# Routing on un-normalised rows in a two-layer mixture-of-experts trunk

## The chip, the cores and the metric

The kernel runs on one core of a Trainium2 chip. TensorE (PE) multiplies, VectorE (DVE) and ScalarE (ACT) work on elements, GpSimd (POOL) does small work and issues its own DMA queue with the gathers and scatters, and SyncE (SP) issues the DMAs that load weights. The metric is device time in microseconds, median over runs.

## The reference, cut to what matters

Two layers. Each is a token mixer (layer 0: stick-breaking attention beside retention; layer 1: differential attention), an output projection, a normalised residual, and then a mixture of 32 small experts, two for each token. For 1024 tokens of 1024 features, with folded rows and columns written out:

```python
y   = ALPHA * x + g1 * (mix @ w_out)              # output projection and residual
n   = (y - mean(y)) * rsqrt(var(y) + eps)         # LayerNorm, without gain and bias
x1  = n * lg + lb                                 # residual that the experts' results are added to
u2  = n * sc + sh                                 # rows that the experts read
lgt = n @ (gain * [w_group | w_router]) + br      # 4 + 32 router logits of a token
group = argmax(lgt[:4]); two best of the group's 8 experts; gates by softmax
x2  = LayerNorm(ALPHA * x1 + g2 * sum over the two experts(gate * expert(u2)))
```

An expert is a gated MLP with 512 hidden units. All arithmetic is float32; the matmuls run as three passes over high and low parts.

## The kernel before, in words

A layer has two stages here. In the first, the class `OutProj` computes the output projection in 8 blocks of 128 tokens, as a generator (`gen`) whose steps are laid between those of the mixer's last head. For each block it runs matmuls over 8 slices of the contraction and two halves of the columns (L511); the last block's remaining 12 matmuls come at the end. VectorE scales the result from PSUM (L515) and adds the residual (L517 in layer 1, L519 in layer 0), then takes statistics (L574). `norm` finishes them: bn_aggr (L580), a reciprocal square root in 12 small operations (`rsqrt`, L162 to L171), the negated scaled mean (L583), and then ScalarE normalises the block in place (L584).

From the normalised block come three things:

- `expert_rows` (L598, L599): u2, two VectorE operations over 128 x 1024 and a store by SP's queue;
- `turn` and `logits` (L607, L623): eight transposes on TensorE, two copies by ScalarE, eight matmuls of 36 columns (TensorE shows each as two), and the bias added by VectorE (L625);
- `residual` (L617): x1, two VectorE operations, and a store by POOL's queue (L618).

After every second block `choose` picks group and experts (L634 to L685), `rank` counts by matmul how many earlier tokens each expert has (L693, L695), `hots` and `place` (L701 to L726) put the tokens into a table of slots, and L1644 makes it a table of integers. What a block leaves to do gets a due time in `put_off`: a count of matmul steps of the projection. A scheduler then orders each engine's instructions from this program order and its own cost estimates. `tc.issue_after` adds an ordering and nothing else.

The second stage, `experts`, runs over a list of jobs p. For each, POOL gathers the rows of its tokens (`gather`, L1385) into a buffer from `xgs`, TensorE transposes them (`x_T`, L1396), ScalarE and VectorE split them into high and low parts (L178, L179), and TensorE multiplies with the expert's weights, which stream in 1 MB pieces through a ring of buffers and are split in the same way (L1434 up, L1479 down). The first gather needs the table and all stored u2. Two of the buffers in `xgs` are the tiles `t_v` that hold the two rows lg and lb during the first stage; they come free when the last `residual` has read them, and are cleared by POOL (L1839) ahead of their gather. x1 of blocks 0 to 5 is made as the blocks come; that of block 6 with the last rows, and that of block 7 (`residual(NB - 1)`) has its first operation behind the slot codes (`coded`) and its second behind `plan.behind`: in layer 0 the first job's transposed rows (`es[0].turned`), in layer 1 the counted table (`plan.tabled`).

Of the kernel before, what the change touches and what calls it, by code (L numbers as in the profile page):

```python
# [12 lines left out]
I32 = mybir.dt.int32  # L13
# [21 lines left out]
def tile_trunk(ctx, tc, x, c, ln1_g, ln1_b, ln2_g, ln2_b, w_ada, b_ada,  # L35
# [28 lines left out]
    def bank1():  # L64
        return psB.tile([P, 512], F32, name="psb")
# [93 lines left out]
    def rsqrt(pool, v, n, tag):  # L159
# [12 lines left out]
        return y  # L172

# [209 lines left out]
    class OutProj:  # L383
# [30 lines left out]
        def open(self, pool, mr, uT, u2, g1, extra, arena, lrows, wr):  # L414
# [18 lines left out]
            self.mv = pool.tile([P, NB, 2], F32, name="ln_mv")  # L433
# [5 lines left out]
        def router(self, wr):  # L439

# [15 lines left out]
            nc.vector.tensor_tensor(self.wf, raw, gain, op=OP.mult)  # L456
            self.vals1 = wr[0][:, 0:4 * NE].rearrange("p (k c e) -> p k c e", k=2, c=2)
# [96 lines left out]
        def put_off(self, b, end):  # L554

            g = [g for g in GROUPS if b in g][0]
            todo = [(9, lambda: self.turn(b)), (12, lambda: self.logits(b))]
            if b < NB - 2:
                todo.insert(1, (9, lambda: self.residual(b)))
            elif b == NB - 1:  # L560
                todo.insert(1, (9, lambda: self.last_rows(end)))
            if b == g[-1]:
                todo += [(12, lambda: self.choose(g)), (17, lambda: self.rank(g)), (17, lambda: self.hots(g)),
                         (21, lambda: self.place(g))]
            self.later += [(2 * KT * (b + 1) + n + (13 if b == NB - 2 else 0), f) for n, f in todo]
            self.later.sort(key=lambda t: t[0])
# [9 lines left out]
        def norm(self, b):  # L576
            y = self.y[b % NY]
            st6 = self.small("st6", [2, 6])
            mv = self.mv[:, b, :]
            nc.vector.bn_aggr(mv, st6)  # L580
            rs = rsqrt(self.pool, mv[:, 1:2], 1, "ln")
            nb = self.small("nb", [1])
            end = nc.vector.scalar_tensor_tensor(nb, mv[:, 0:1], -1.0, rs, op0=OP.mult, op1=OP.mult)  # L583
            nc.scalar.activation(y, y, AF.Identity, bias=nb, scale=rs)  # L584
            if b < NB - 2:
                self.expert_rows(b)
            self.put_off(b, end)
# [22 lines left out]
        def residual(self, b):  # L610
            y = self.y[b % NY]
            for i, (t, op) in enumerate(zip(self.lrows, (OP.mult, OP.add))):
                with ExitStack() as st:
                    if b == NB - 1:

                        st.enter_context(tc.issue_after((self.coded, self.rt.plan.behind)[i].ins))
                    nc.vector.tensor_tensor(y, y, t, op=op)  # L617
            nc.gpsimd.dma_start(x1_d[self.l][b * P:(b + 1) * P, :], y)  # L618

        def logits(self, b):  # L620
# [4 lines left out]
            nc.vector.tensor_tensor(self.small("lg", [GM, 36])[:, b - g[0], :], pl[:, 0:36], self.br, op=OP.add)  # L625

        def choose(self, g):
# [44 lines left out]
            nc.vector.tensor_tensor(oh_all[:, b0:b0 + n, :], oh[:, :, 0, :], oh[:, :, 1, :], op=OP.add)  # L672
# [24 lines left out]
        def hots(self, g):  # L697
# [3 lines left out]
            nc.vector.tensor_tensor(rj, self.oh, self.pr[:, 0:n * NE].rearrange("p (b e) -> p b e", b=n).unsqueeze(2)  # L701
                                    .broadcast_to([P, n, 2, NE]), op=OP.mult)
# [1089 lines left out]
    def experts(l, rt, dst):  # L1792

        with ExitStack() as st:
# [68 lines left out]
            rt.op.residual(NB - 1)  # L1863
# [375 lines left out]
```

## Time and profile before

| what | value |
|---|---|
| median of 3 runs | 2659.84 us (2657.39 to 2667.03) |
| profiled execution | 2662.61 us |
| its span, first to last instruction | 2660.9 us |
| PE busy | 2432.1 us (91%) |
| DVE busy | 1788.2 us (67%) |
| ACT busy | 1080.7 us (41%) |
| POOL busy | 341.5 us (13%) |
| mean granted TensorE clock | 0.949 |

The first stage of layer 0 ends near 740 us and that of layer 1 near 1980 us of the span; the experts follow. A busy share of 91% is a mean over stretches that are full and stretches, at the two joints, in which TensorE waits and its clock is lowered, so the joints have to be read by themselves. The median lies 2.8 us below the profiled execution.

### The profile page before, as it was taken

Reading aid. Unit: us, or ns where it says so; the run is one execution under the profiler, and the core shown is the slowest. Engines: PE = TensorE matmul, PEld = TensorE weight load, DVE = VectorE, ACT = ScalarE, POOL = GpSimd, SP = SyncE. Lnnn points to the kernel's source line nnn. Section 1 sums busy time; section 2 is a strip of 40 time slices with the busy share of each in tenths; the row PEclk is TensorE's granted clock in tenths of the full one; section 3 lists DMA queues with packets and bytes.
Section 4 is the critical chain, followed back from the end, with each engine's and each line's share of the span. In section 5 each row is a group of like instructions: output and inputs, shape, how many; then the busy total and the mean of one; then the engine's idle time right before and its main releaser. Section 6 shows DMA issues by size and latency. Waiting matters only on the chain. (4 is left out here: it accounts for less than half of the span.)

```text
span 2660.9 us, 37454 instructions
## 1 busy us (share of the span) xinstructions
PE 2432.1 (91%) x13530; PEld 1800.6 (68%) x13530; DVE 1788.2 (67%) x3659; ACT 1080.7 (41%) x1806; POOL 341.5 (13%) x286
## 2 busy tenths in 40 slices
PE   6999999989889999999879999999979999989995
PEld 5776678877767544445468898987767766656651
DVE  6678987768888564555476778788877545453446
ACT  3344542222267433444354545454226432332331
POOL 1000001110022211222100000000011121121211
PEclk9999999999989999999979999999979999999996
DMA  7534455533579989999833334233268998997983
GB/s 237 146 92 119 120 137 171 170 116 123 206 287 379 369 327 383 388 383 390 315 142 93 92 76 117 64 112 121 101 225 315 372 347 295 408 406 267 381 340 136
DMA packets 216802, 616.65 MB, mean 232 GB/s; under 512 B 31872, under 2 KB 111928, under 8 KB 167457
## 3 DMA queue, kind: packets, MB, share of 16 engines
q1 hardware_dynamic: 193312, 555.96, 57.1%
q0 software_dynamic: 23296, 58.20, 8.7%
q8 instruction: 110, 1.80, 0.3%
q14 instruction: 84, 0.68, 0.1%
HBM read 555.67 MB, written 60.80 MB: 232 GB/s over the span
## 5 line engine op out<-in xcount | busy, mean ns | idle before, releaser
L228 PE MATMUL psb<-w_b,w_sp 128*128 128x512 f32 x1536 | 402.3, 404 | 0.0
L179 DVE TENSOR_TENSOR e_lo<-w_b,e_hi 128x1024 fp32r<-128x1024 f32 x256 | 303.5, 1221 | 79.0 <-ACT e_hi L178 77.3
L178 ACT CAST e_hi<-w_b 128x1024 fp32r<-128x1024 f32 x256 | 261.1, 1047 | 137.9 <-PE psb L1434 71.8
L228 PEld LDWEIGHTS psb<-w_b,w_sp 128*128 128x128 f32 x1536 | 279.9, 191 | 52.5 <-issue 0.7
L248 PE MATMUL psb<-w_sp,w_b 128*128 128x256 f32 x1824 | 248.7, 288 | 0.3
L248 PEld LDWEIGHTS psb<-w_sp,w_b 128*128 128x128 f32 x1824 | 227.7, 191 | 3.2 <-issue 1.2
L1434 PE MATMUL psb<-e_hi,w_sp 128*128 128x512 f32 x592 | 201.6, 410 | 0.6 <-ACT e_hi L178 0.6
L1434 PE MATMUL psb<-e_hi,e_x 128*80 128x512 f32 (+2 forms) x576 | 187.4, 400 | 1.2 <-issue 1.1
L123 DVE SCALAR_TENSOR_TENSOR ada_acc<-ada_slab,cond,ada_acc 128x512 f32<-128x512 f32 x160 | 125.0, 781 | 57.2 <-DMA ada_slab<-in_w_ada_dram 53.9
L511 PE MATMUL psb<-w_b,w_sp 128*128 128x512 f32 x576 | 150.7, 410 | 6.3 <-ACT w_sp L178 6.3
L1492 POOL DMA_INDIRECT x_d<-e_y,tabi x38 | 101.9, 2682 | 411.2 <-DVE e_y L1486 371.7
L1434 PEld LDWEIGHTS psb<-e_hi,w_sp 128*128 128x128 f32 x592 | 115.7, 195 | 31.4 <-ACT e_hi L178 3.5
L1434 PE MATMUL psb<-e_lo,w_sp 128*128 128x512 f32 x320 | 131.0, 409 | 6.5 <-DVE e_lo L179 6.5
L1479 PE MATMUL psa<-e_hi,e_hh 128*128 128x512 f32 (+3 forms) x304 | 128.8, 425 | 4.3 <-ACT e_hi L178 4.1
L1479 PE MATMUL psa<-e_lo,e_hh 128*128 128x512 f32 (+3 forms) x304 | 131.2, 432 | 1.2 <-DVE e_lo L179 1.2
L1322 ACT ACTIVATE df_z<-df_z,df_nm 128x256 f32<-128x256 f32 (+7 forms) x128 | 98.3, 769 | 82.5 <-DVE df_nm L1320 72.0
L1479 PE MATMUL psa<-e_hi,e_hl 128*128 128x512 f32 (+3 forms) x304 | 128.3, 423 | 0.0
L511 PEld LDWEIGHTS psb<-w_b,w_sp 128*128 128x128 f32 x576 | 108.8, 195 | 28.8 <-ACT w_sp L178 6.9
L1434 PE MATMUL psb<-e_lo,e_x 128*80 128x512 f32 (+2 forms) x288 | 116.1, 403 | 11.1 <-DVE e_lo L179 11.1
L1434 PEld LDWEIGHTS psb<-e_hi,e_x 128*80 128x80 f32 (+2 forms) x576 | 96.4, 168 | 38.8 <-issue 2.0
L1385 POOL DMA_INDIRECT t_v<-u_d,tabi x70 | 83.6, 1194 | 230.3 <-PE psa L1512 164.4
L1028 DVE TENSOR_TENSOR_SCAN t_keep<-t_keep,zero 128x128 f32<-128x128 f32 (+7 forms) x64 | 86.7, 1355 | 25.5 <-ACT t_keep L1018 25.1
(544 smaller groups left out, 4729.9 us busy)
## 6 DMA issues: line engine op xcount, KB each, us to landing
w_b<-in_moe_w_dram SPq DMA_DIRECT2D x261, 1024.0 KB
w_raw<-in_moe_w_dram SPq DMA_DIRECT2D x60, 1024.0 KB
w_sp<-in_moe_w_dram SPq DMA_DIRECT2D x44, 1024.0 KB
ada_slab<-in_w_ada_dram SPq DMA_DIRECT2D x160, 256.0 KB
e_ring<-in_moe_w_dram SPq DMA_DIRECT2D x17, 1024.0 KB
w_raw<-in_even_w_in_dram SPq DMA_DIRECT2D x24, 512.0 KB
ada_slab<-in_w_ada_dram SPq DMA_DIRECT2D x16, 512.0 KB
x_d<-w_raw POOLq DMA_DIRECT2D x16, 512.0 KB, 3.1
```

The costliest lines, as they stand in the source:

```text
L123: nc.vector.scalar_tensor_tensor(acc, slab, cond[:, k:k + 1], acc, op0=OP.mult, op1=OP.add)
L178: nc.scalar.copy(hi, src)
L179: return eng.tensor_tensor(lo, src, hi.bitcast(F32), op=OP.subtract)
L228: nc.tensor.matmul(ps, s[:, k % 4, cs], m[:, k, :], start=k == 0 and j == 0, stop=k == KT - 1 and j == 2)
L248: nc.tensor.matmul(ps[:, t, :], s[:, k, sl], m[:, k % 4, :], start=k == 0 and j == 0, stop=k == KT - 1 and j == 2)
L511: nc.tensor.matmul(pss[b][n], m[:, s, k, :], self.wo[k][:, w, ns], start=k == 0 and j == 0, stop=k == KT - 1 and j == 2)
L1028: nc.vector.tensor_tensor_scan(R[:, ::-1], R[:, ::-1], zero1.broadcast_to([P, W]), 1.0, OP.mult, OP.add)
L1322: nc.scalar.activation(pm[m][:, 0:W], pm[m][:, 0:W], AF.Exp, bias=nm[:, m:m + 1], accum_out=H.ss[:, qb, m:m + 1])
L1385: self.gathered = nc.gpsimd.indirect_dma_start(out=xg[0:m], out_offset=None, in_=u2_d[self.l], in_offset=bass.IndirectOffsetOnAxis(ap=tab[ ...
L1434: self.upped = nc.tensor.matmul(ps[0:n], s[:, ks], wt[:, ws], start=k == 0 and j == 0, stop=k == KT - 1 and j == len(sms) - 1)
L1479: nc.tensor.matmul(pn, s[:, ks], w[:, ns], start=k == 0 and j == 0, stop=k == 3 and j == 2)
L1492: nc.gpsimd.indirect_dma_start(out=x1_d[self.l], out_offset=bass.IndirectOffsetOnAxis(ap=tab[0], axis=0), in_=y, in_offset=None, bounds_ch ...
```

## The change

The router works on y itself, not on n. As the mean times a column sum is what the normalisation takes away, the columns of the weights are made free of their mean once for each layer (three more VectorE operations, one matmul), and the logits are then rs * (y @ wf) + br, with rs the reciprocal square root of the token. ScalarE's normalising pass is gone. The rows u2 and x1 take the norm in with them: (y - mean) * row0, then * rs + row1, as two operations that read a scalar of each token and a second tensor (`row_step`). The reciprocal square root of a block has 9 small operations instead of 12 and L583.

The due times are smaller (turn 3, logits 6, rows 6, residual 9; before 9, 12, none, 9), and block 6's are put off by 7, not 13. The rows of blocks 6 and 7 and their residuals, which stood together behind block 7's norm, now stand in different places: rows of block 6 behind block 7's reciprocal square root, rows of block 7 behind the choice (`chosen`) and ahead of `hots`, the first residual operation of block 6 behind `coded`, and the other three behind `plan.behind`.

```diff
+            nc.vector.tensor_reduce(s, self.wf.rearrange("p k n -> p n k"), axis=AX.X, op=OP.add)
+            nc.tensor.matmul(ps[:, 0:36], ones, s, start=True, stop=True)
+            nc.vector.tensor_scalar(s, ps[:, 0:36], -1.0 / D, None, op0=OP.mult)
+            nc.vector.tensor_tensor(self.wf, self.wf, s.unsqueeze(1).broadcast_to([P, KT, 36]), op=OP.add)
...
-            todo = [(9, lambda: self.turn(b)), (12, lambda: self.logits(b))]
+            todo = [(3, lambda: self.turn(b)), (6, lambda: self.logits(b))]
             if b < NB - 2:
-                todo.insert(1, (9, lambda: self.residual(b)))
-            elif b == NB - 1:
-                todo.insert(1, (9, lambda: self.last_rows(end)))
+                todo += [(6, lambda: self.expert_rows(b)), (9, lambda: self.residual(b))]
+            if b == NB - 1:
+                todo += [(6, lambda: self.last_rows(NB - 2, self.scaled))]
             if b == g[-1]:
+                todo += [(12, lambda: self.choose(g))]
+                if b == NB - 1:
+                    todo += [(12, lambda: self.last_rows(NB - 1, self.chosen))]
...
         def norm(self, b):
-            rs = rsqrt(self.pool, mv[:, 1:2], 1, "ln")
-            end = nc.vector.scalar_tensor_tensor(nb, mv[:, 0:1], -1.0, rs, op0=OP.mult, op1=OP.mult)
-            nc.scalar.activation(y, y, AF.Identity, bias=nb, scale=rs)
+            self.rs[b], self.scaled = rsqrt1(self.rt.pool, mv[:, 1:2], f"ln{b % 2}")
...
+        def row_step(self, i, b, out_, y, rows):
+            if i == 0:
+                return nc.vector.scalar_tensor_tensor(out_, y, self.mv[:, b, 0:1], rows[0], op0=OP.subtract, op1=OP.mult)
+            return nc.vector.scalar_tensor_tensor(out_, out_, self.rs[b], rows[1], op0=OP.mult, op1=OP.add)
...
-            rt.op.residual(NB - 1)
+            rt.op.residual(NB - 2, (rt.op.coded, plan.behind))
+            rt.op.residual(NB - 1, (plan.behind, plan.behind))
```

The lines move: L584 is gone, and the changed kernel's L533 is L511 of before (matmuls of the projection), L628 is L607 (transposes), L643 and L645 are L623 and L625 (logits and what finishes them), L614 and L615 are the two row steps in place of L598, L599 and L617, L638 is L618 (store of x1), L1409 is L1385 (gather), L1863 is L1839 (clearing a gather's buffer).

Three places show what moves. First TensorE at the end of layer 0's projection, before: w_b are its weights, w_sp the mixed heads, w_raw the rows y, t_q their transposes, ada_slab the router's weights.

```order
L511 MATMUL psa<-w_b_5510,w_sp 128x512 [waits Activation_49]
L511 MATMUL psa<-w_b_5510,w_sp 128x512
L511 MATMUL psa<-w_b_5510,w_sp 128x512 [waits DVE_49]
L511 MATMUL psa<-w_b_5509,w_sp 128x512 [waits DVE_49]
L511 MATMUL psa<-w_b_5509,w_sp 128x512 x5
L511 MATMUL psa<-w_b_5510,w_sp 128x512 x6
L607 MATMUL psb<-identf,w_raw 128x128 [waits Activation_49]
L607 MATMUL psb<-identf,w_raw 128x128 x3
L607 MATMUL psb<-identf,w_raw 128x128 [waits PE_49]
L607 MATMUL psb<-identf,w_raw 128x128 x3
L623 MATMUL psb<-ada_slab,t_q 128x36 [waits Activation_49]
```

The same place in the changed kernel:

```order
L1104 MATMUL psb<-identf,t_k 128x128 [waits PE_49]
L643 MATMUL psb<-ada_slab,t_q 128x36 [waits DVE_49,Activation_49]
L643 MATMUL psb<-ada_slab,t_q 128x36 x3
L643 MATMUL psb<-ada_slab,t_q 128x36 [waits Activation_49]
L643 MATMUL psb<-ada_slab,t_q 128x36 x2
L533 MATMUL psa<-w_b_5510,w_sp 128x512 [waits Activation_49]
L533 MATMUL psa<-w_b_5510,w_sp 128x512
L533 MATMUL psa<-w_b_5510,w_sp 128x512 [waits DVE_49]
L643 MATMUL psb<-ada_slab,t_q 128x36
L533 MATMUL psa<-w_b_5509,w_sp 128x512 [waits DVE_49]
L533 MATMUL psa<-w_b_5509,w_sp 128x512 x5
L533 MATMUL psa<-w_b_5510,w_sp 128x512 x6
```

The last 12 projection matmuls (two rows, of 5 and 6, with one before them) stood ahead of block 6's transposes and logits; now block 6's logits, and its transposes above the rows shown, stand ahead of them, and so does a transpose of the head.

Second, VectorE between block 7's reciprocal square root and the choice of layer 0, before: t_qw is the output of u2 rows, w_sp and t_v the folded rows, t_g small tiles, psb the logits in PSUM.

```order
L583 SCALAR_TENSOR_TENSOR t_g<-ln_mv,ln_i 128x1 [waits DVE_49]
L598 TENSOR_TENSOR t_qw<-w_raw,w_sp 128x1024 [waits DMAHW2_49]
L599 TENSOR_TENSOR t_qw<-t_qw,w_sp 128x1024 [waits DVE_49]
L598 TENSOR_TENSOR t_qw<-w_raw,w_sp 128x1024 [waits Activation_49]
L617 TENSOR_TENSOR w_raw<-w_raw,t_v 128x1024
L599 TENSOR_TENSOR t_qw<-t_qw,w_sp 128x1024 [waits DVE_49]
L617 TENSOR_TENSOR w_raw<-w_raw,t_v 128x1024 [waits DVE_49]
L625 TENSOR_TENSOR t_g<-psb,ada_slab 128x36 [waits PE_49]
L634 TENSOR_REDUCE t_g<-t_g 128x2 [waits DVE_49]
L636 TENSOR_TENSOR t_g<-t_g 128x8 [waits DVE_49]
```

In the changed kernel:

```order
L186 SCALAR_TENSOR_TENSOR ln_i<-ln_t,ln_i 128x1 [waits DVE_49]
L614 SCALAR_TENSOR_TENSOR t_qw<-w_raw,ln_mv,w_sp 128x1024 [waits DMAHW2_49]
L645 SCALAR_TENSOR_TENSOR t_g<-psb,ln_i,ada_slab 128x36 [waits DVE_49,PE_49]
L615 SCALAR_TENSOR_TENSOR t_qw<-t_qw,ln_i,w_sp 128x1024 [waits DVE_49]
L655 TENSOR_REDUCE t_g<-t_g 128x2 [waits DVE_49]
L657 TENSOR_TENSOR t_g<-t_g 128x8 [waits DVE_49]
```

Six row operations stood between the norm and the logits of block 7; now it is one, and one more behind the logits, ahead of the choice's first operation. The two rows of block 7 have moved behind the choice and the residual steps further down.

Third, POOL's queue at the start of layer 0's experts, before: u_d holds the rows u2, t_v are gather buffers, x_d holds x1.

```order
L1385 DMA t_v<-u_d_72,tabi_133 128x1024 [waits DMAHW3_49,DMAHW4_49,DMAHW2_49,DMAHW6_49,DMAHW1_49,DMAHW7_49,DMASW7_49,DVE_49]
L1846 MEMSET mark_6925 128x1 [waits DMAHW0_49,DMAHW5_49,PE_49,DMAHW6_49,Activation_49,Pool_49]
L1839 MEMSET t_v 128x1024
L1677 MEMSET pl_ones 32x128
L1385 DMA t_v<-u_d_72,tabi_133 128x1024 [waits DMASW0_49,Pool_49]
L1385 DMA t_v<-u_d_72,tabi_133 128x1024 [waits DMASW7_49,DMASW1_49,PE_49]
L1839 MEMSET t_v 128x1024 [waits DVE_49]
L618 DMA x_d_78<-w_raw 128x1024 [waits DMASW2_49]
L1385 DMA t_v<-u_d_72,tabi_133 128x1024 [waits DMASW3_49,Pool_49]
```

In the changed kernel:

```order
L1409 DMA t_v<-u_d_72,tabi_133 128x1024 [waits DMAHW4_49,DMAHW3_49,DMAHW5_49,DMAHW2_49,DMAHW6_49,DMAHW1_49,DMAHW7_49,DMASW6_49,DVE_49]
L1870 MEMSET mark_6887 128x1 [waits DMASW7_49,PE_49,DMAHW0_49,Activation_49,Pool_49]
L1701 MEMSET pl_ones 32x128
L1409 DMA t_v<-u_d_72,tabi_133 128x1024 [waits DMASW6_49,PE_49]
L638 DMA x_d_78<-w_raw 128x1024 [waits DMASW0_49,DVE_49]
L1863 MEMSET t_v 128x1024 [waits DVE_49]
L1409 DMA t_v<-u_d_72,tabi_133 128x1024 [waits DMASW1_49,Pool_49]
L1863 MEMSET t_v 128x1024 [waits DVE_49]
L638 DMA x_d_78<-w_raw 128x1024 [waits DMASW2_49]
L1409 DMA t_v<-u_d_72,tabi_133 128x1024 [waits DMASW3_49,Pool_49]
```

The second gather, that of job 1, stood right behind the first with its buffer cleared in between; it is now the one behind the first L1863, which waits for VectorE, and both the gather that waits for TensorE and the store of block 6's x1 stand ahead of it. The first gather is the first row in both, the gather that waits for TensorE the one with PE in its waits.

## Rows read from the trace of the kernel before

**Rows 1.** Windows: us, busy (x instructions) of PE, PEld, DVE, ACT, POOL; PEclk, DMA share, GB/s

```profile
680.00:700.00 20.00, 19.96 (x108) 16.88 (x106) 17.38 (x49) 4.79 (x6) 0.53 (x1) 1.00 0.30 97
720.00:740.00 20.00, 11.93 (x71) 10.34 (x69) 15.23 (x53) 4.83 (x8) 0.53 (x1) 0.67 0.93 356
...
800.00:850.00 50.00, 50.00 (x236) 37.61 (x235) 44.22 (x42) 35.03 (x38) 8.85 (x6) 1.00 1.02 381
1960.00:1980.00 20.00, 11.10 (x79) 10.39 (x78) 16.50 (x66) 4.35 (x7) 1.06 (x2) 0.55 0.72 268
```

**Rows 2.** PE's waits, 700 to 760 us: us in total, times, longest

```profile
PE psb L693 <- DVE oh_all L672: 5.5, 2, 3.6
PE psa L1396 <- DMA t_v<-u_d,tabi: 4.7, 1, 4.7
PE psb L607 <- ACT w_raw L584: 4.0, 1, 4.0
```

**Rows 3.** PE's waits, 1815 to 1945 us

```profile
PE psb L607 <- ACT w_raw L584: 2.3, 1, 2.3
```

**Rows 4.** Timeline of PE, end of layer 0's projection: start, us, [idle before <-releaser]

```profile
717.57 5.46 PE L511 MATMUL psa<-w_b,w_sp 128*128 128x512 f32 x12 [1.51 <-DVE w_raw L519]
722.85 1.06 PE L607 MATMUL psb<-identf,w_raw 128*128 128x128 f32 x8
724.20 1.97 PE L623 MATMUL psb<-ada_slab,t_q 128*128 128x36 f32 x16 [0.29 <-ACT t_q L608]
732.03 3.63 PE L623 MATMUL psb<-ada_slab,t_q 128*128 128x36 f32 x16
...
759.67 1.06 PE L1396 MATMUL psa<-identf,t_v 128*128 128x128 f32 x8
```

**Rows 5.** Timeline of DVE, 724 to 756 us

```profile
724.52 0.69 DVE L574 BATCH_NORM_STATS2 t_g<-w_raw 128x6 f32<-128x512 f32 x1
...
735.93 0.16 DVE L634 TENSOR_REDUCE t_g<-t_g 128x2 f32<-128x8 f32 x1
...
738.94 0.23 DVE L672 TENSOR_TENSOR oh_all<-t_g 128x64 bf16<-128x64 f32 x1
...
739.82 0.29 DVE L701 TENSOR_TENSOR t_g<-t_g,psb 128x128 f32<-128x128 f32 x1
...
751.13 1.23 DVE L179 TENSOR_TENSOR e_x<-psa,e_x 128x1024 fp32r<-128x1024 f32 x1 [2.46 <-ACT e_x L178]
```

**Rows 6.** DVE, all operations of L851 (two tensors, one scalar): ns min/median/max, first to last start

```profile
L851 DVE SCALAR_TENSOR_TENSOR ada_acc<-ada_slab,cond,ada_acc x16: 1274/1284/3243, 9.1 to 41.5; 128x1024 f32<-128x1024 f32 x16
```

**Rows 7.** Timeline of POOL, 742 to 757 us

```profile
743.59 1.09 POOL L1385 DMA_INDIRECT t_v<-u_d,tabi  x1 [6.98 <-DMA w_raw<-in_moe_w_dram]
...
753.54 0.95 POOL L1839 MEMSET t_v<- 128x1024 f32 x1 [2.23 <-DVE w_raw L617]
...
755.35 1.33 POOL L1385 DMA_INDIRECT t_v<-u_d,tabi  x1 [0.31 <-issue]
```

**Rows 8.** L1385, issued 740 to 800 us: from issue to landing

```profile
DMA to landing us min/median/max: 4.4/8.4/13.5
```

**Rows 9.** L1385, issued 755 to 756 us: from issue to landing

```profile
DMA to landing us min/median/max: 7.4/7.4/7.4
```

**Rows 10.** Timelines of DVE, POOL and PE, layer 1, 1955 to 2001 us

```profile
1957.62 0.69 DVE L574 BATCH_NORM_STATS2 df_q<-w_raw 128x6 f32<-128x512 f32 x1
...
1969.62 0.16 DVE L634 TENSOR_REDUCE df_q<-df_q 128x2 f32<-128x8 f32 x1
...
1992.56 0.19 DVE L1713 TENSOR_REDUCE pl_full<-pl_v 128x1 f32<-128x32 f32 x1
...
1996.07 1.06 POOL L1385 DMA_INDIRECT t_v<-u_d,tabi  x1 [0.17 <-POOL bt_iota L1580]
...
1999.16 1.05 PE L1396 MATMUL psa<-identf,t_v 128*128 128x128 f32 x8
```

**Rows 11.** L1385, issued 1996 to 1997 us: from issue to landing

```profile
DMA to landing us min/median/max: 9.3/9.3/9.3
```

More of the change, by code (lines that the diff above doesn't have):

```diff
@@ L172, in rsqrt, with rsqrt1 @@
         return y
+    def rsqrt1(pool, v, tag):
+        nh = pool.tile([P, 1], F32, name=tag + "_h")
+        nc.vector.tensor_scalar(nh, v, EPS, -0.5, op0=OP.add, op1=OP.mult)
+        yi = pool.tile([P, 1], I32, name=tag + "_i")
+        nc.vector.tensor_scalar(yi, nh.bitcast(I32), 1, None, op0=OP.arith_shift_right)
+        nc.vector.tensor_scalar(yi, yi, -1.0, float(0x5F3759DF - 0x400000 - 0x40000000), op0=OP.mult, op1=OP.add)
+        y = yi.bitcast(F32)
+        t = pool.tile([P, 1], F32, name=tag + "_t")
+        for _ in range(3):
+            nc.vector.tensor_scalar(t, y, y, nh, op0=OP.mult, op1=OP.mult)
+            end = nc.vector.scalar_tensor_tensor(y, t, 1.5, y, op0=OP.add, op1=OP.mult)
+        return y, end
     rsqrt_end = [None]
@@ L432, in open @@
             self.router(wr)
-            self.mv = pool.tile([P, NB, 2], F32, name="ln_mv")
+            self.mv = self.rt.pool.tile([P, NB, 2], F32, name="ln_mv")
+            self.rs = {}
             self.arena = [(t, [0]) for t in arena]
@@ L608, in turn, with residual @@
                 nc.scalar.copy(uT[:, 4 * h:4 * h + 4, :].rearrange("p k t -> p (k t)"), pt)
-        def residual(self, b):
+        def residual(self, b, behind=(None, None)):
             y = self.y[b % NY]
-            for i, (t, op) in enumerate(zip(self.lrows, (OP.mult, OP.add))):
+            for i in range(2):
                 with ExitStack() as st:
-                    if b == NB - 1:
-                        st.enter_context(tc.issue_after((self.coded, self.rt.plan.behind)[i].ins))
-                    nc.vector.tensor_tensor(y, y, t, op=op)
+                    if behind[i]:
+                        st.enter_context(tc.issue_after(behind[i].ins))
+                    self.row_step(i, b, y, y, self.lrows)
             nc.gpsimd.dma_start(x1_d[self.l][b * P:(b + 1) * P, :], y)
@@ L624, in logits @@
             g = [g for g in GROUPS if b in g][0]
-            nc.vector.tensor_tensor(self.small("lg", [GM, 36])[:, b - g[0], :], pl[:, 0:36], self.br, op=OP.add)
+            nc.vector.scalar_tensor_tensor(self.small("lg", [GM, 36])[:, b - g[0], :], pl[:, 0:36], self.rs[b], self.br,
+                                           op0=OP.mult, op1=OP.add)
         def choose(self, g):
@@ L2154, in route @@
         rt = Route()
+        rt.pool = pool
         rt.plan = Plan(l, rt, pool, NSTAT[l], SIZES[l])
```

36 lines of the change are left out of this document (16 added, 20 removed).

## The prediction

> **What bounds the kernel now.** I read the windows first. Inside the first stage and in the experts TensorE is full: 19.96 of 20 us in 680 to 700, all 50 us in 800 to 850, where the DMA engines are full as well (share 1.02) [rows 1]. At the two joints it isn't: 11.93 of 20 us at a granted clock of 0.67 in 720 to 740, and 11.10 at 0.55 in 1960 to 1980 [rows 1]. A change of norm and routing acts on the time there, or where TensorE waits for the norm inside the first stage. The waits say for what: at the joint of layer 0 it waits 5.5 us for the choice (longest 3.6), 4.7 for the first gathered rows and 4.0 for ScalarE's normalising pass [rows 2]; among the earlier blocks I count one wait for that pass worth naming, 2.3 us in layer 1 [rows 3]. Then the timelines give the chain of the joint. Block 7's rows y are complete when its statistics start, at 724.52; the choice starts at 735.93, its result is there at 738.94, the first gather is issued at 743.59, and job 1's rows are transposed at 759.67 [rows 4, 5, 7]. VectorE, not TensorE, sets 735.93: six row operations run between the norm and the logits, though TensorE ends the logits at 735.66 as well, because its clock is low (the 16 logits matmuls of block 7 take 3.63 us, those of block 6 1.97) [rows 4].
>
> **The change part by part.** All sums are in the profiled execution, 2662.61 us, of which 1.7 lie outside the span; the median of the runs is 2.8 lower, and so is my forecast for it.
>
> *Blocks 0 to 5.* The ACT pass and four small operations of a block leave the path to the transposes. Worth at most the 2.3 us of [rows 3]; the mean-free weights add three small operations and a matmul per layer, ahead of the first block where VectorE has time, at most 1 us if uncovered. The 64 row operations become a form with two tensors and a scalar. The same form over 128x1024 takes 1.284 us in L851 [rows 6]; a plain two-tensor operation of that size takes 1.23 [rows 5]. So 64 times 0.05 is 3 us on VectorE, in stretches where it has 17.38 of 20 us taken and TensorE is full [rows 1]: hidden. I take -1.5, between -2.3 and +1.
>
> *Joint of layer 0, up to the first gather.* Block 6's transposes and logits, 722.85 to 726.17, so 3.3 us [rows 4], now stand ahead of the last 12 projection matmuls. These took 5.46 us at the low clock, behind a wait of 1.51 [rows 4]. With that work in the wait's place I expect them at the upper level, near half, 2.7 us. Complete rows y then come 0.6 later (725.1); at the low clock 3.3 later (727.8). I take 725.8. From there, turn and logits of block 7 take 3.3 us as block 6's did at the upper clock. VectorE beside it has the statistics (0.69) and some eleven small operations at about 0.2 with their gaps (L634 is 0.16 long) [rows 5], 2.9 us together by this estimate, and one row operation of block 6, until 730.0. So the logits are finished at 730.2, the second row operation of block 6 follows (1.28), and the choice starts at 731.5 instead of 735.93: -4.4. With TensorE at the low clock it would be about -3.
>
> Two row operations of block 7 now stand between the choice's result and the use of the ranks: 2 x 1.28 + 0.3 where 0.88 passed before (738.94 to 739.82 [rows 5]), so +2.0. The table and the first gather come 2.4 earlier, at 741.2. But block 7's store, and the 3 MB of weights that wait for it, leave about 3 us later than before, so they run beside the gather. It landed in 4.4 us; the five gathers of this stretch took 4.4 to 13.5, median 8.4 [rows 8]. I take 6.4: the first rows are transposed only 0.4 earlier.
>
> *Joint of layer 0, the second gather.* This is where the change adds a wait. Job 1's buffer is one of the tiles that hold lg and lb. Before, its clearing and gather came right behind the first. Now the tile is read until block 7's first residual operation, which is placed behind the first job's transposed rows. Block 6's second operation and block 7's first run behind the split e_x (751.13 [rows 5], now 750.7): 1.2 + 2 x 1.28, so until 754.5. Then POOL clears the buffer (0.95 [rows 7]) and issues at 755.5, past the store of block 6's x1, which stands ahead in its queue. Behind this gather there wait a clearing, the second x1 store and the next gather. The gather that POOL issued at 755.35 took 7.4 us [rows 9]; with that, job 1's rows are there at 762.9. TensorE asked for them at 759.67 [rows 4]; the new order puts three matmuls more ahead of it (0.7 us, by their rate of 0.23 at the upper clock), so its own time would be 760.4. Late by +2.5 against before. By 4.4 us it would be no loss (-0.4), by 13.5 it would be +8.6. Three row operations among the splits of e_lo, where one stood, cost up to 2.6 us on VectorE; they delay the first job's matmuls ahead of the same gather, so they are no term of their own.
>
> *Joint of layer 1.* The choice started at 1969.62, 12.0 us after block 7's rows were complete (1957.62) [rows 10]. Now block 6's transposes and logits (3.3) stand ahead of the 12 matmuls, which makes 1960.9, and 5.7 us later, as in layer 0, the choice: 1966.6, so -3.0, and +2.0 for block 7's rows: -1.0. Between -2.3 and +1.5, the upper end with TensorE at the low clock. The second gather waits here for the counted table (last operation 1992.56 [rows 10], now 1991.7), two row operations (2.6) and a clearing (0.95): issue at 1995.3. That is the place of the gather of 1996.07, which took 9.3 us [rows 10, 11]: 2004.6. TensorE transposed job 1's rows at 1999.16 [rows 10], now some 1.1 later for matmuls moved ahead. Late by +4.3; by 4.4 us -0.6, by 13.5 +8.5.
>
> *Sum.* Joints +6.8. TensorE and the DMA engines are both full in the experts [rows 1], so no view says which of them carries a late start to the end: if TensorE, all of it; if the weights, that go on filling their ring meanwhile, less. I let 5 of 6.8 through. -1.5 + 5 = +3.5: 2666.1 for the profiled execution, 2663 for the median.
>
> **The rivals.** *A, the joints pay.* Both gathers land about as fast as the first one, 4.4 us. Then layer 0 gets its 2.4, layer 1 its 1.0, the blocks 2.3: -5.7, so 2654. For it: the late gathers are issued when the 3 MB are mostly in. Against it: four of the five gathers in the stretch were slower than that one, which went first [rows 8].
>
> *B, POOL's queue piles up, slower.* The second gather now goes out beside x1 stores, a weight piece on the same queue and the ring's pieces. If gathers there take 13.5 us, the slowest seen [rows 8], TensorE's stall is +8.6 in layer 0 and +8.5 in layer 1, all carried: 2676. It decides from landings of some 12 us on, in both layers. Against it: the gathers at just these places took 7.4 and 9.3.
>
> *C, the row operations run at half rate.* The L851 row gives 1.284 us for 1024 elements of each partition, as fast as the plain form to 5% [rows 6]. The Trainium skill (Vector Engine (DVE) Microarchitecture Reference, section 7, Points that are easy to get wrong) says that a scalar-tensor-tensor with two non-bf16 sources in SBUF runs at half throughput. By that rule the operation would take twice what a two-tensor one takes; L851's sources are two f32 tensors too, and its row disagrees with it here. Were the row steps at 2.5 us all the same, 64 of them would add 79 us to VectorE, which has 2.6 us of 20 free in the first stage [rows 1]; with half of it hidden, 2700.
>
> **How the numbers follow.** My forecast 60%, its own range 2657 to 2669 (the late gathers 2 us faster or 2.5 us slower in both layers). A 27%, B 11%, C 2%. The range takes in A with its spread down to 2650 and goes up to 2672, where B's lower part begins; B's rest, C and the low edge of A stay outside. 0.5% is 13.3 us, about what a measurement tells from no change: below 2646.5 or above 2673.1. Faster by that needs both joints at their lower bounds (-3.1 or so each), the blocks at theirs and more: 4%. Slower: most of B and C and a little of my own case's tail, 11%. The rest, 85%, lies within.
>
> **What would show it.** Right: TensorE has no wait for ScalarE ahead of L628 any more; layer 0's choice (L655) starts near 6 us behind block 7's complete rows, where 11.4 passed before; the first gather goes out 1 to 3 us earlier; TensorE waits 2 to 5 us at L1420 for job 1's rows in both layers, and the gathers there have landed 7 to 10 us after their issue. L614 and L615 take near 1.28 us. Wrong: no wait for job 1's rows (then A), landings of 12 us and a wait for job 2's rows as well (B), L614 over 2 us (C). If the 12 matmuls still run at 0.455 us each, my time for the choice is too early by 2 to 3 us; if the start of the experts moves by 5 us and the end doesn't, it was the weights that set the end.

## The result, and the profile after

| | before | changed kernel |
|---|---|---|
| median of 5 runs, us | 2659.84 (2657.39 to 2667.03) | 2685.60 (2676.64 to 2688.58) |
| profiled execution, us | 2662.61 | 2676.64 |
| span, us | 2660.9 | 2674.9 |

The ratio of the times is 1.0072, 95% interval 1.0046 to 1.0097: slower by some 19 us, and above the forecast's whole range. (The quotient of the two medians, 1.0097, is higher.) The changed kernel's five times fall into two groups, 2676.64 and 2676.69 and then 2685.60 to 2688.58; the profiled execution is of the first, 9 us below the median.

The first row of the statistics in each layer's projection cuts the span into parts that can be compared. VectorE's timeline of before:

```profile
609.67 0.69 DVE L574 BATCH_NORM_STATS2 t_g<-w_raw 128x6 f32<-128x512 f32 x1
...
1830.51 0.69 DVE L574 BATCH_NORM_STATS2 df_q<-w_raw 128x6 f32<-128x512 f32 x1
```

From there to there it is 1220.84 us, and 830.4 from the second row to the end of the span. VectorE's timeline of the changed kernel, with the joint of layer 0 between the two rows and that of layer 1 behind them:

```profile
605.54 0.69 DVE L598 BATCH_NORM_STATS2 t_g<-w_raw 128x6 f32<-128x512 f32 x1
...
719.82 0.69 DVE L598 BATCH_NORM_STATS2 t_g<-w_raw 128x6 f32<-128x512 f32 x1
...
725.30 0.15 DVE L655 TENSOR_REDUCE t_g<-t_g 128x2 f32<-128x8 f32 x1
...
728.29 0.22 DVE L693 TENSOR_TENSOR oh_all<-t_g 128x64 bf16<-128x64 f32 x1
...
737.48 0.16 DVE L1662 MEMSET few_o<- 64x1 f32 x2 [2.06 <-DMA u_d<-t_qw]
...
749.61 1.22 DVE L194 TENSOR_TENSOR e_lo<-w_b,e_hi 128x1024 fp32r<-128x1024 f32 x1
750.74 1.28 DVE L615 SCALAR_TENSOR_TENSOR w_raw<-w_raw,ln_i,t_v 128x1024 f32<-128x1024 f32 x1
751.94 5.76 DVE L194 TENSOR_TENSOR e_lo<-w_b,e_hi 128x1024 fp32r<-128x1024 f32 x5
...
1836.10 0.69 DVE L598 BATCH_NORM_STATS2 df_q<-w_raw 128x6 f32<-128x512 f32 x1
...
2002.59 5.76 DVE L194 TENSOR_TENSOR e_lo<-w_b,e_hi 128x1024 fp32r<-128x1024 f32 x5
```

Layer 0's part takes 1230.56 us now, 9.7 more, and layer 1's 838.8, 8.4 more: 18 us, most of them, by the next table, lost where the experts begin. (What precedes 605.54 is not touched by the change and came 4.1 us earlier in this execution.) The 8.4 is no measure of what layer 1 loses: from job 4's rows, in the last line of the next table, to the end of the span it is 597.6 us here and 603.6 before. The work there is the same; TensorE's mean granted clock is not, 0.91 before and 0.96 after in these two windows, each 400 us behind those rows, before and then after (columns as in [rows 1]):

```profile
2457.00:2537.00 80.00, 73.90 (x399) 50.02 (x392) 37.77 (x40) 29.34 (x38) 15.90 (x11) 0.91 0.99 376
```

```profile
2477.00:2557.00 80.00, 77.55 (x432) 52.35 (x435) 36.69 (x38) 29.23 (x38) 15.98 (x11) 0.96 0.99 385
```

Why it differs is open. The places of the joint, each counted from the layer's first statistics:

| us from the layer's first statistics | layer 0 before | after | layer 1 before | after |
|---|---|---|---|---|
| block 7's rows y complete (its statistics start) | 114.9 | 114.3 | 127.1 | 131.3 |
| choice starts | 126.3 | 119.8 | 139.1 | 137.2 |
| first gather issued | 133.9 | 133.0 | 149.0 | 149.3 |
| first job's rows transposed | 138.4 | 137.5 | 152.9 | 152.5 |
| job 1's rows transposed | 150.0 | 160.4 | 168.7 | 180.8 |
| later job (job 3 in layer 0, job 4 in layer 1) | 182.0 | 193.5 | 226.8 | 241.2 |

Up to the first job nothing is lost; between the first job and job 1 it is 11 to 13 us in each layer. TensorE's waits of the changed kernel (us in total, times, longest), layer 0's joint and then layer 1's, say for what:

```profile
PE psa L1420 <- DMA t_v<-u_d,tabi: 18.7, 2, 10.8
PE psb L714 <- DVE oh_all L693: 8.5, 2, 5.3
...
PE psa L1420 <- DMA t_v<-u_d,tabi: 12.1, 2, 11.1
```

Gathered rows cost 18.7 us in two waits where they cost 4.7 in one [rows 2]. The second of the two is job 1's, as TensorE's timeline shows in both layers:

```profile
713.99 4.34 PE L533 MATMUL psa<-w_b,w_sp 128*128 128x512 f32 x12 [1.40 <-DVE w_raw L541]
...
743.03 1.97 PE L1420 MATMUL psa<-identf,t_v 128*128 128x128 f32 x8 [7.88 <-DMA t_v<-u_d,tabi]
...
765.90 1.97 PE L1420 MATMUL psa<-identf,t_v 128*128 128x128 f32 x8 [10.79 <-DMA t_v<-u_d,tabi]
...
2016.90 1.95 PE L1420 MATMUL psa<-identf,t_v 128*128 128x128 f32 x8 [11.15 <-DMA t_v<-u_d,tabi]
```

Before, it transposed these rows when it came to them [rows 4, 10]. POOL's timeline of the changed kernel holds the reason:

```profile
738.50 1.10 POOL L1409 DMA_INDIRECT t_v<-u_d,tabi  x1 [41.00 <-DVE pl_gt L1690]
...
745.28 1.05 POOL L1409 DMA_INDIRECT t_v<-u_d,tabi  x1 [5.42 <-PE psa L1420]
748.79 0.60 POOL L638 DMA_DIRECT2D x_d<-w_raw  x1 [2.47 <-DVE w_raw L615]
749.76 0.95 POOL L1863 MEMSET t_v<- 128x1024 f32 x1 [0.36 <-DVE w_raw L614]
750.98 7.63 POOL L1409 DMA_INDIRECT t_v<-u_d,tabi  x1 [0.27 <-POOL t_v L1863]
758.60 0.97 POOL L1863 MEMSET t_v<- 128x1024 f32 x1
759.50 0.60 POOL L638 DMA_DIRECT2D x_d<-w_raw  x1
760.40 1.05 POOL L1409 DMA_INDIRECT t_v<-u_d,tabi  x1 [0.30 <-issue]
...
2001.63 7.63 POOL L1409 DMA_INDIRECT t_v<-u_d,tabi  x1 [0.27 <-POOL t_v L1863]
```

Job 1's gather begins at 750.98, 12.5 us behind the first; before it was 2.4. And the instruction itself takes 7.63 us, where the first takes 1.10, in both layers alike. It ends at 758.61 and 2009.26; VectorE's row of five e_lo splits, shown above, ends at 757.70 and 2008.35: 0.91 us earlier, in both. The landings of these two gathers, from the start of the instruction:

```profile
DMA to landing us min/median/max: 14.9/14.9/14.9
...
DMA to landing us min/median/max: 15.1/15.1/15.1
```

Counted from the end of the instruction that is 7.3 and 7.5 us, between the 6.1 and 8.2 that the gathers of [rows 7, 9] and [rows 10, 11] give in the same way (7.4 less 1.33, 9.3 less 1.06). Windows of the changed kernel, same stretches and columns as [rows 1]:

```profile
680.00:700.00 20.00, 19.96 (x102) 16.75 (x101) 17.34 (x34) 2.23 (x4) 1.06 (x2) 1.00 0.36 136
720.00:740.00 20.00, 6.46 (x63) 5.83 (x63) 15.34 (x65) 3.79 (x7) 1.36 (x3) 0.59 0.98 388
```

ScalarE has 2.23 us where it had 4.79, VectorE as much as before: the norm left ScalarE and cost VectorE nothing here.

### The profile page after: what moved, and what is told of

Read it like the earlier page. It is cut to its first block, busy times and chain, and to the rows that moved or that the text cites. A ratio compares the mean times of both kernels' runs of the same rounds, so it can differ in the third digit from the quotient of the medians.

```text
span 2674.9 us, 37387 instructions
## 1 busy us (share of the span) xinstructions
PE 2424.3 (91%) x13534; PEld 1795.8 (67%) x13534; DVE 1782.4 (67%) x3601; ACT 1062.4 (40%) x1790; POOL 363.8 (14%) x286
## 5 line engine op out<-in xcount | busy, mean ns | idle before, releaser
L1516 POOL DMA_INDIRECT x_d<-e_y,tabi x38 | 109.4, 2878 | 402.7 <-DVE e_y L1510 363.1
L533 PE MATMUL psb<-w_b,w_sp 128*128 128x512 f32 x576 | 150.6, 407 | 4.9 <-ACT w_sp L193 4.9
L1409 POOL DMA_INDIRECT t_v<-u_d,tabi x70 | 99.0, 1415 | 296.0 <-PE psa L1536 158.6
L1458 PE MATMUL psb<-e_lo,e_x 128*80 128x512 f32 (+2 forms) x288 | 116.9, 406 | 11.1 <-DVE e_lo L194 11.1
L533 PEld LDWEIGHTS psb<-w_b,w_sp 128*128 128x128 f32 x576 | 107.0, 193 | 26.3 <-ACT w_sp L193 5.4
```

The source lines that it names most:

```text
L533: nc.tensor.matmul(pss[b][n], m[:, s, k, :], self.wo[k][:, w, ns], start=k == 0 and j == 0, stop=k == KT - 1 and j == 2)
L1409: self.gathered = nc.gpsimd.indirect_dma_start(out=xg[0:m], out_offset=None, in_=u2_d[self.l], in_offset=bass.IndirectOffsetOnAxis(ap=tab[ ...
L1458: self.upped = nc.tensor.matmul(ps[0:n], s[:, ks], wt[:, ws], start=k == 0 and j == 0, stop=k == KT - 1 and j == len(sms) - 1)
L1516: nc.gpsimd.indirect_dma_start(out=x1_d[self.l], out_offset=bass.IndirectOffsetOnAxis(ap=tab[0], axis=0), in_=y, in_offset=None, bounds_ch ...
```

## The experiments

Times are medians, each compared with the kernel before on the same chip; every interval is for 95%.

| run | us | before | ratio | y complete, L0 / L1 | job 1's rows, L0 / L1 |
|---|---|---|---|---|---|
| changed kernel | 2685.60 | 2659.84 | 1.0072 [1.0046, 1.0097] | 114.3 / 131.3 | 160.4 / 180.8 |
| e1 | 2664.87 | 2663.46 | 1.0008 [0.9993, 1.0022] | 115.7 / 132.5 | 150.2 / 170.1 |
| e2 | 2680.19 | 2663.46 | 1.0062 [1.0040, 1.0083] | 117.6 / 132.5 | 155.1 / 174.2 |
| e3 | 2679.51 | 2663.46 | 1.0053 [1.0034, 1.0073] | 116.4 / 127.9 | 152.0 / 166.1 |
| e4 | 2652.63 | 2663.46 | 0.9958 [0.9945, 0.9971] | 108.8 / 123.5 | 143.4 / 160.7 |
| e5 | 2653.63 | 2664.51 | 0.9964 [0.9950, 0.9978] | 108.6 / 123.4 | 143.3 / 160.9 |
| e6 | 2650.34 | 2664.51 | 0.9944 [0.9931, 0.9958] | 108.7 / 123.8 | 144.0 / 162.8 |
| e7 | 2667.81 | 2664.51 | 1.0012 [1.0001, 1.0023] | 116.9 / 132.6 | 151.8 / 172.4 |
| e8 | 2650.03 | 2664.51 | 0.9944 [0.9931, 0.9957] | 108.7 / 123.8 | 143.2 / 162.0 |

The last two columns are counted as in the table above.

**e1: only block 7's first residual operation goes back behind the slot codes.**

```diff
-            rt.op.residual(NB - 1, (plan.behind, plan.behind))
+            rt.op.residual(NB - 1, (rt.op.coded, plan.behind))
```

> The changed kernel with one edit: block 7's first residual operation stands behind the slot codes again, so that the buffer of job 1's gather is free early. Theory 1 (the loss is job 1's gather: its buffer is held by block 7's residual, and then POOL's gather instruction is kept up by VectorE's row of split operations): the gather instruction takes 1.0 to 1.4 us instead of 7.63, TensorE waits under 2 us for job 1's rows in both layers instead of 10.8 and 11.1, and the time is 2645 to 2660, below before by up to 12. Theory 2 (the loss is in the new row operations or their places on VectorE): no gain, 2673 to 2690. Theory 3 (gathers land late in this stretch whatever their place, from the weights' traffic): TensorE still waits 5 us or more for job 1's rows; 2665 to 2680.

The loss is gone, 1.0072 to 1.0008, though not in the range that theory 1 had (2645 to 2660): this run is level with before, not below. TensorE has no wait for job 1's rows in either layer. POOL's timeline of layer 0 has job 1's gather 2.4 us behind the first again, at its usual length:

```profile
744.51 1.10 POOL L1409 DMA_INDIRECT t_v<-u_d,tabi  x1 [40.90 <-DVE pl_gt L1690]
...
746.93 1.06 POOL L1409 DMA_INDIRECT t_v<-u_d,tabi  x1 [0.17 <-POOL pl_ones L1701]
```

The place of one VectorE operation, whose result only the second residual operation and the store of x1 need, is worth about 17 us. The operation itself takes 1.28 us in each layer, so most of that is what waits for the buffer that it reads. In layer 1 the gain is smaller: job 4's rows come 235.7 us behind the first statistics, where the changed kernel has 241.2 and before 226.8. Job 2's gather is held there for 5.47 us, and TensorE waits 5.5 us for it.

**e2: the splits of e_lo are kept off the gather.** The buffer is still held, but VectorE's row of splits starts only behind a mark that POOL writes after job 1's gather.

```diff
+                if p == 1:
+                    with tc.issue_after(es[1].gathered.ins):
+                        nc.gpsimd.memset(mark[2], 0.0)
+                    plan.second = nc.vector.tensor_copy(mark[3], mark[2])
...
-                            st.enter_context(tc.issue_after(E.turned.ins))
+                            st.enter_context(tc.issue_after(plan.second.ins))
```

> The changed kernel, with the splits of job 0's remaining weights placed behind job 1's gather on VectorE (a small mark that POOL writes behind the gather and VectorE copies). The buffer is held as long as in the changed kernel; only VectorE's unbroken row of operations no longer runs beside the gather. Theory 1 in its second half (VectorE keeps up the gather instruction): it takes 1.0 to 1.4 us on POOL instead of 7.63, lands 4 to 9 us after its issue instead of 14.9, TensorE's wait for job 1's rows falls to 1 to 5 us in each layer, and the time to 2660 to 2672 though VectorE idles some 2 us. Rival (the instruction waits for room in the DMA queue behind the x1 store, or for something in memory): it stays near 7.6 us and the time at 2675 to 2692.

POOL's timeline (job 1's gather of layer 0, job 2's of layer 1), and then TensorE's waits of layer 0 and of layer 1 and its timeline in layer 1:

```profile
757.82 1.06 POOL L1409 DMA_INDIRECT t_v<-u_d,tabi  x1 [0.31 <-issue]
...
2001.94 1.47 POOL L1409 DMA_INDIRECT t_v<-u_d,tabi  x1 [0.30 <-issue]
```

```profile
PE psb L1458 <- DVE e_lo L194: 2.7, 1, 2.7
...
PE psb L1458 <- DVE e_lo L194: 4.2, 1, 4.2
```

```profile
2018.32 0.48 PE L1420 MATMUL psa<-identf,t_v 128*128 128x128 f32 x1 [9.70 <-DMA t_v<-u_d,tabi]
```

Job 1's gather takes 1.06 us with VectorE quiet and lands in 4.4 (layer 1: 1.07 and 4.2), so without the row of splits beside it, it isn't held. (It need not be held beside one: the next gather, at 760.16, took 1.06 beside four splits.) The time, though, hardly moved: TensorE now waits for the later splits and, in layer 1, 9.7 us for the rows of job 2. Their gather goes out 24 us behind the first instead of 17, and it lands late as well, with a short instruction:

```profile
DMA to landing us min/median/max: 16.3/16.3/16.3
```

The expectation of the time was missed. As the later splits are this run's own cost, it doesn't tell what the long instruction alone is worth; e3 has the hold without it.

**e3: the kernel before with that hold and nothing else.**

```diff
-                        st.enter_context(tc.issue_after((self.coded, self.rt.plan.behind)[i].ins))
+                        st.enter_context(tc.issue_after(self.rt.plan.behind.ins))
```

> The kernel before with one edit: block 7's first residual operation stands behind the first job's transposed rows (layer 0) or the counted table (layer 1), as in the changed kernel; all else as before. Theory 1: this alone makes the loss. Job 1's gather goes out 8 to 12 us later than before in layer 0, its instruction takes 4 to 8 us, TensorE waits 6 to 14 us for job 1's rows in each layer; 2672 to 2692. Theory 2 (the loss is in the row operations and where they stand): within 5 us of before, 2655 to 2665.

It loses 0.53%, without the new norm, router or due times. POOL's timeline in layer 1 and TensorE's wait there:

```profile
1995.82 1.86 POOL L1385 DMA_INDIRECT t_v<-u_d,tabi  x1 [0.27 <-POOL t_v L1839]
...
2012.20 0.54 POOL L1368 DMA_DIRECT2D w_raw<-in_moe_w_dram  x1 [8.78 <-DMA x_d<-w_raw]
2013.04 1.78 POOL L1385 DMA_INDIRECT t_v<-u_d,tabi  x1 [0.31 <-issue]
```

```profile
PE psa L1396 <- DMA t_v<-u_d,tabi: 13.6, 2, 11.5
```

The time is as theory 1 had it, but not by its steps: job 1's gather takes only 1.86 us (expected 4 to 8), and TensorE waits 0.5 us for job 1's rows in layer 0 and 2.1 in layer 1 (expected 6 to 14). What is late is the queue behind it. A weight load on POOL's queue waits 8.78 us for a store of x1, and job 2's gather stands behind it, 30 us behind the first gather instead of 17. TensorE waits 11.5 us for it.

**e4: norm and router alone.** The changed kernel's `rsqrt1`, `row_step` and mean-free router, with the due times and the places of the last rows of before.

```diff
-            todo = [(3, lambda: self.turn(b)), (6, lambda: self.logits(b))]
+            todo = [(9, lambda: self.turn(b)), (12, lambda: self.logits(b))]
...
-                    todo += [(12, lambda: self.last_rows(NB - 1, self.chosen))]
...
-            rt.op.residual(NB - 2, (rt.op.coded, plan.behind))
-            rt.op.residual(NB - 1, (plan.behind, plan.behind))
+            rt.op.residual(NB - 1, (rt.op.coded, plan.behind))
```

> The changed router, reciprocal square root and row operations, but with the due times and the places of the last blocks' rows and residuals of the kernel before. Theory 1: no loss; the wait of TensorE for ScalarE's normalising pass is gone (4.0, 4.3 and 2.3 us before), the row operations of blocks 6 and 7 still hold up the choice; 2652 to 2660. Theory 2 (the row operations cost the time): 2668 to 2690.

It is 0.42% faster than before, about 11 us, and the gain comes earlier than at the joint: rows y are complete 6.1 us sooner in layer 0 and 3.6 in layer 1. TensorE's timeline of before, ahead of [rows 4]:

```profile
710.88 0.18 PE L693 MATMUL psb<-oh_all,trib 128*128 128x32 bf16 x1 [1.93 <-DVE oh_all L672]
...
712.62 0.65 PE L724 MATMUL psb<-t_g 128*128 128x64 f32 x2 [1.32 <-DVE t_g L708]
```

That is the ranking of blocks 4 and 5, for which TensorE waits 1.93 and 1.32 us; the 12 matmuls behind it then take 5.46 [rows 4]. In e4:

```profile
706.49 0.19 PE L716 MATMUL psb<-oh_all,trib 128*128 128x32 bf16 x1
...
714.40 3.01 PE L533 MATMUL psa<-w_b,w_sp 128*128 128x512 f32 x12
```

No wait for the ranking, and the same 12 in 3.01 us. The windows of before (700 to 725) and of e4 (700 to 720) have the granted clock at 0.80 and 1.00:

```profile
700.00:725.00 25.00, 19.91 (x96) 15.82 (x96) 16.84 (x66) 3.68 (x8) 0.53 (x1) 0.80 0.72 281
```

```profile
700.00:720.00 20.00, 18.62 (x110) 15.39 (x109) 16.95 (x62) 1.85 (x5) 0.53 (x1) 1.00 0.96 360
```

1.93 + 1.32 + 2.45 (the 12 matmuls) is 5.7 of the 6.1 us. The choice of blocks 4 and 5 has its result 94.1 us behind the first statistics in e4, 100.9 before; how much of that is ScalarE's pass and how much the shorter reciprocal square root was not tested.

**e5: e1 with the due times of before.** As e4's first two lines, on e1; the last rows stay spread as in the change.

> The run with block 7's first residual operation early (e1), and in addition the due times of the kernel before (turn 9, logits 12, rows with the norm, residual 9, block 6 put off by 13). Rows of block 7 stay behind the choice. It stands between e1 (2664.9 us) and e4 (2652.6). Theory 4: the new due times cost what e1 lost against e4, because block 6's transposes and logits and the slot work of blocks 4 and 5 come ahead of the last projection matmuls: block 7's rows are then complete 109 and 124 us behind the first statistics of their layer (e4: 108.8 and 123.5; e1: 115.7 and 132.5), time 2648 to 2657. Theory 5: block 7's rows behind the choice cost it, as their late store holds the first gather: block 7's rows complete early all the same, but the time stays at 2660 to 2667.

0.9964, as expected by theory 4: as fast as e4 within the intervals, and 0.44% below e1. So spreading the last rows neither pays nor costs once block 7's first operation is in its old place, and the new due times cost.

**e7: e4 with the new due times, the other way round.** The edit is e4's first pair of lines undone, with the rows of blocks 0 to 5 put off to 6 and block 6 by 7.

> e4 (new router, norm in the rows, places of the last rows as before; 2652.6 us) with the new due times alone. Theory 4: block 7's rows complete at 114 and 131 us behind the first statistics instead of 108.8 and 123.5, time 2659 to 2669. Theory 5: no change against e4 beyond 3 us, 2649 to 2656.

1.0012 against e4's 0.9958: they cost about 14 us of themselves, and hid e4's gain in the changed kernel. TensorE's timeline of e7:

```profile
706.84 0.18 PE L714 MATMUL psb<-oh_all,trib 128*128 128x32 bf16 x1 [3.20 <-DVE oh_all L693]
...
711.87 3.08 PE L643 MATMUL psb<-ada_slab,t_q 128*128 128x36 f32 x14
...
717.92 4.85 PE L533 MATMUL psa<-w_b,w_sp 128*128 128x512 f32 x12 [1.27 <-DVE w_raw L541]
```

The choice of blocks 4 and 5 has its result 99.2 us behind the first statistics, 5 us later than in e4; why the due times delay it was not taken apart. TensorE waits 3.20 us for it, block 6's logits stand ahead of the last 12 matmuls, and these take 4.85 us again.

**e6 and e8: parts of the spreading on e4.** e6 puts block 7's two rows behind the choice, e8 takes block 6's residual out of the way of the choice:

```diff
+                if b == NB - 1:
+                    todo += [(12, lambda: self.rows7())]
```

```diff
-                self.residual(NB - 2)
...
+            rt.op.residual(NB - 2, (rt.op.coded, plan.behind))
             rt.op.residual(NB - 1, (rt.op.coded, plan.behind))
```

> e4 with block 7's two row operations behind the choice, ahead of the use of the ranks, as in the changed kernel. Both theories say that the choice starts some 2.5 us earlier in each layer. Theory 5: the first gather then waits for the store of block 7's rows, 9 to 10 us after the choice's result instead of 5.5, so it goes out 1 to 3 us later than in e4 relative to block 7's complete rows: 2654 to 2664. If the store doesn't hold it, the gather goes out about as in e4: 2649 to 2655.

> e4 with block 6's two residual operations taken from ahead of the choice: the first behind the slot codes, the second where block 7's second stands; stores of rows as in e4. If VectorE sets the start of the choice, it starts 2 to 2.5 us earlier in each layer and the first gather with it: 2646 to 2652. If the logits on TensorE or the store of block 7's rows set it, no gain: 2651 to 2656.

Both come to 0.9944, 0.14% below e4, with intervals that overlap e4's: too little to tell. The choice starts 6.7 (e6) and 8.0 us (e8) behind the complete rows, where e4 has 10.3. In layer 0 the first gather then comes 8.4 and 7.1 behind the choice's result where e4 has 5.5, so it gives back most of what the choice gained. In layer 1 it is 9.0 and 6.8 where e4 has 6.8: e6 gives it back there too, e8 doesn't. e8, at 2650.03 us, is faster than both kernels, by 0.56% [0.43, 0.69] than the one before.

**e9 and e10: which operations hold a gather.** On e2, 12 f32 operations stand in place of the splits beside job 1's gather, adding two tensors (e9) or summing one (e10). The result is not used.

```diff
+                    plan.second = nc.vector.tensor_tensor(g2[:, h:h + 512], y7[:, h:h + 512], y6[:, h:h + 512], op=OP.add)
```

```diff
+                    plan.second = nc.vector.tensor_reduce(g2[:, j:j + 1], y7[:, h:h + 512], axis=AX.X, op=OP.add)
```

> A measurement of the disputed cost, in the run with the splits behind the second gather (e2), where that gather's instruction took 1.06 us beside an idle VectorE. Here VectorE runs an unbroken row of 12 additions of two SBUF tensors (128x512, about 0.6 us each, their result is not used) beside it. If VectorE's row holds the instruction: it takes 5 to 9 us on POOL and ends about when the row does, in both layers, as in the changed kernel. If the instruction in the changed kernel waited for something else: 1.0 to 1.9 us, whatever VectorE does. The whole time is of no interest: some 10 us over e2 by the added work.

> As e9, with 12 sums over one SBUF tensor (128x512 to 128x1) in place of the 12 additions of two, so VectorE is as busy beside the gather but reads one tensor. If it is the second tensor of VectorE's row that holds POOL's instruction: 1.0 to 1.4 us. If any unbroken row on VectorE does: 5 to 9 us, as in e9.

VectorE's timeline of e9, then POOL's:

```profile
756.25 7.31 DVE L1897 TENSOR_TENSOR e_g<-w_raw 128x512 f32<-128x512 f32 x12
...
2009.32 4.63 DVE L194 TENSOR_TENSOR e_lo<-w_b,e_hi 128x1024 fp32r<-128x1024 f32 x4
```

```profile
757.38 1.11 POOL L1409 DMA_INDIRECT t_v<-u_d,tabi  x1 [0.31 <-issue]
...
2011.40 3.47 POOL L1409 DMA_INDIRECT t_v<-u_d,tabi  x1 [0.30 <-issue]
```

Beside 7.31 us of two-tensor adds the gather takes 1.11 us, so by e9's own criterion such a row doesn't hold it. In the same run a gather beside four e_lo splits takes 3.47 and ends at 2014.87, 0.92 behind the end of that row (2013.95). e10's gather beside the sums takes 1.06 us, and its later one beside splits 3.80, again ending 0.92 behind the row. So neither two source tensors nor a busy VectorE was enough here. It is three gathers in each run that passed (1.10 and 1.11 us in e9, 1.03 to 1.06 in e10), and some pass beside splits as well, so that such rows can never hold a gather is not shown. What is particular to the splits (an fp32r result, 1024 columns, the tensors they read) was not taken apart and stays open. Times, 2679.71 and 2680.10 us (ratios 1.0062 [1.0044, 1.0080] and 1.0055 [1.0041, 1.0069]), are e2's.

## Why the prediction was wrong, point by point

- **The second gather: the step that failed.** Its place was right. By the working, job 1's gather starts 145.8 and 164.8 us behind the first statistics; it was 145.4 and 165.5. Its price was not: "with that, job 1's rows are there at 762.9", by 7.4 and 9.3 us from issue to landing, for +2.5 and +4.3. Measured are landings of 14.9 and 15.1, and job 1's rows 10.4 and 12.2 us later than before. The sum took POOL's instruction as 1 us of work, as all its rows show it (1.06 to 1.33 in [rows 7, 10]); it was held for 7.63. The rows of before did not show the hold: the two gathers I took the price from ran beside e_lo splits as well and were not held. The changed kernel against e1 shows that this step, with what is queued behind it, makes 0.64% of the 0.72%; e3 shows that the hold alone slows the kernel before as well.
- **What is queued behind it** was named in the prediction (a clearing, a store, the next gather) and put at nothing. e2 and e3 show that the hold is worth nearly as much without a long instruction: with gathers of 1.06 and 1.86 us they still lose 0.62% and 0.53%, e2 in part by its own later splits.
- **Rival B** came nearest: slower by 16 us, against 19 measured, and its condition, landings above 12 us in both layers, was met. Its 2676 stands on the scale of the median, which was 2685.60; that the profiled execution took 2676.64 is chance. Its mechanism was landings that are slow beside other transfers. For job 1 the rows show something else, 7.3 and 7.5 us of landing behind an instruction that ended late, and its other sign, a wait for job 2's rows, is absent from the changed kernel. Late landings of that kind do show in e2: 16.3 us behind an instruction of 1.47.
- **Blocks 0 to 5, "I take -1.5".** e4 shows about -11 for norm and router, the last blocks included. I looked only for waits for ScalarE's pass and not for what it delays: the choice of blocks 4 and 5, TensorE's wait for it and the clock behind it. The due times then cost about 14 us (e7 against e4; 12 by e1 against e5), where I had 0.6 and 3.3 us for block 6's work at the joints. The two errors hid each other, and it is luck that block 7's rows came within 2 us of my times in layer 0 (114.3, forecast 116.1) and within 1 in layer 1 (131.3, forecast 130.4).
- **The 12 projection matmuls** were forecast at 2.7 us for layer 0; they took 4.34. e4's 3.01 is the time without TensorE's waits for the ranking.
- **The choice** was right: 5.5 and 5.9 us behind the complete rows, forecast 5.7. **The first gather** was not: rows of block 7 were priced at +2.0, but the gather came 10.2 us behind the choice's result instead of 4.65, 5.6 more. VectorE's row at 737.48 ends a wait for a store of u2. Block 7's is the last, issued behind the second row operation, which ends at 731.2; the table of integers was done at 735.3, so the gather of 738.50 did not wait for it. As it then landed in 4.5 us, the first job's rows came 0.9 earlier, forecast 0.4.
- **What gets through.** 5 of 6.8 were let through, 74%. From the later job's delay to the layer's end it was 9.7 of 11.5 us in layer 0. In layer 1 it was 8.4 of 14.4, but in an execution whose tail ran 6 us faster by itself; in e1 and e3 the end came later than before by 9.8 and 15.2 us, where job 4's rows were 8.9 and 11.9 late. So more gets through than I let.
- **The row operations (rival C)** took what L851 did:

```profile
L614 DVE SCALAR_TENSOR_TENSOR w_raw<-w_raw,ln_mv,t_v x16: 1273/1278/1286, 608.6 to 1999.1; 128x1024 f32<-128x1024 f32 x16
```

Put together by ratios: e5 against before, the norm with the rows spread, is -0.36%; the due times (e1 against e5) +0.44%; the held buffer (the changed kernel against e1) +0.64%. That is +0.72%, the measured loss; as each step is taken between neighbours of one chain, the sum comes out by itself and confirms nothing. What does is that each part was measured a second way: the norm without the spread rows (e4) is -0.42%, the due times on it (e7 against e4) +0.54%, the hold on the kernel before (e3) +0.53%, together +0.65%.

## What to carry to other kernels

Before an operation nobody waits for is moved later, look up which tile it is the last to read and who wants that tile: its price is the transfer that fills the tile next, with all that stands behind it in that queue. Two rows in which an instruction got past a busy neighbour (1.33 and 1.06 us here) are no bound for the third (7.63). And lay an edit's parts out singly: here a gain of 0.4% was in the change, and two other parts of it, which cost 0.44% and 0.64%, covered it.

## What the runs showed of the hardware

A gather's instruction on POOL takes 1.0 to 1.1 us alone, but beside a row of VectorE's e_lo splits it was held for 3.47 to 7.63 us in seven gathers of six kernels: the changed kernel's two, one each in e9 and e10, and one in layer 1 each of e1, e5 (both 5.47 us) and e8 (4.34). In six of them it ended 0.91 to 0.94 us behind the end of the row, in e8 0.94 behind the last split but one. In e5 and e8 TensorE waits 5.6 and 4.6 us for the rows of the held gather, and both are faster than before all the same.

Not every gather beside such a row is held: those of 755.35 and 1996.07 before took 1.33 and 1.06 [rows 7, 10], and e3's two 1.87 and 1.86. The three of these that took over 1.1 us end in the same way, but behind a single operation: e3's 0.88 and 0.87 us behind the end of the residual operation that ran when they began, the one of 755.35 0.92 behind the split that did, with the next operation of the row already under way. Read so, a gather here gets through behind the end of one of VectorE's operations, and what varies is how many it misses. What decides that is open.

The Trainium skill (SBUF — State Buffer, Who interferes with whom) says that a VectorE instruction with two SBUF inputs contends with a GpSimd one that reads SBUF, and it infers that a `tensor_tensor` doesn't hold up the generation of a DMA's descriptors. The runs differ from that inference: beside rows of such splits the gather was held, over up to five of them. Whether one of e9's adds (0.68 us) holds a gather until its end, 1.11 us beside 1.05 to 1.10 can't tell.
